# Half of the retention output product by seven products in place of eight, in a two-layer trunk on one core

## The chip, the cores and the metric

The kernel runs on one core of a Trainium2 chip. The metric is the device time of one execution in microseconds. Before the change it is 2571.68 us, the median of three runs (2571.43 to 2574.8). One further execution was profiled; it took 2570.78 us, and its trace spans 2569.0 us from the first to the last instruction.

## The reference

The program is a trunk of two layers over a sequence of 1024 positions with 1024 features. Layer 0 mixes by forgetting attention, layer 1 by retention; each mixer and each feed-forward block (SwiGLU) adds to the residual. The part in question is the end of retention:

```python
    _, y = lax.scan(step, state0, (qc, kc, vc))            # per head: inner + cross
    y = y.transpose(1, 0, 3, 2, 4).reshape(B, S, H, dv)    # H = 4 heads, dv = 512
    mu = jnp.mean(y, axis=-1, keepdims=True)
    var = jnp.mean(jnp.square(y - mu), axis=-1, keepdims=True)
    y = ((y - mu) * lax.rsqrt(var + EPS)).reshape(B, S, H * dv).astype(h.dtype)
    return (jax.nn.silu(g) * y) @ w_out                    # (1024 x 2048) @ (2048 x 1024)
```

So each head gives 512 features per position, normalised over these 512, gated by silu(g), and multiplied by its rows of `w_out`. Four heads make 2048 features, which are 16 feature tiles of 128; heads 0 and 1 are the first eight of them.

## The kernel before

Activations are held transposed: a tile has 128 features in its partitions and 512 positions (one half of the sequence, `H = 512`, called h or ib = 0, 1) along the free axis. Every float32 operand is split into a rounded part and a rest (`hi`, `lo`; ScalarE casts, VectorE subtracts: lines 105 and 106), and a product is three matmuls: hi·hi, hi·lo, lo·hi. A line number is that of the kernel before unless said otherwise.

Retention runs over eight stages (head h, half ib). A stage works in this order: `scores` of the next stage (k times q, L1177 to L1179, then mask and decay on VectorE, L1188 and L1193), `weighted` (v times scores, L1203 to L1205), in the second half `crossed` (state times q, L1214 to L1216), and `finish`. `finish` copies four result banks out (`yt`), squares and adds them (`yacc`, L1233), splits the sum (`ah`, `al`), and adds over the partitions by three matmuls into `sm` (L1238 to L1240); from these come q and fb, and four multiplications `yt * fb` (L1248). For head 0 the gate g is loaded and multiplied there (L1252); for heads 1 to 3 it is multiplied later, in `load_units` (L831), with 1024 columns at once. The result is stored to DRAM as `zd`. `prepare` fetches the next head: kf (k for the transposes L1129), the parts of k and q (L1106, by POOL's queue) and eight v tiles (L1092, by SP's queue, then L1095 and L1096).

The output product then has two halves. The first (heads 0 and 1) takes for each of eight row tiles n a weight of 128x1024, split once, and two halves of eight feature tiles: 8 x 3 matmuls each (`mm_u`, L113 to L115), to which the residual `xo` is added (L1287). The second half (heads 2 and 3) is done by `out_proj` in the same manner, added to the first.

Other products of the kernel already go by seven products of 2x2 blocks (`Products`: matmuls at L675 to L677; `Blocks` forms the sums of the weight's blocks; `Stored` holds the sums of the other operand, B11, B21, B22 as they are and T1 to T4 as sums, in DRAM). For a pair of row tiles and a pair of feature tiles they need 7 products of 128x128x512 where the plain way needs 8.

Tiles come from rings: `units` of the pools bpa (32) and bpb (24) hold the split operands, `yu` 16 tiles of 128x512, `qu` four (`q`; kf lies there too), `st` five of 128x1024, `sc` and `xo` a few. A load waits until the ring's tile has been read for the last time. The order of each engine's instructions is set by the framework's planner, which simulates times while it places them; each engine, and each engine's DMA queue, then works strictly in that order.

Of the kernel before, what the change touches and what calls it, by code (L numbers as in the profile page):

```python
# [17 lines left out]
P = 128  # L18
# [19 lines left out]
def trunk(ctx, tc, nc, d, out):  # L38
# [38 lines left out]
    def yu(s):  # L77
        return yp.tile([P, H], F32, tag="y", name=nm(s))
# [453 lines left out]

    class Combos:
# [74 lines left out]
    class Blocks:  # L608


        def __init__(self, src):
            self.s1, self.ready = None, {}
            sts = []
            for i in range(2):
                st = sp.tile([P, 1024], F32, tag="st", name=nm("st"), bufs=5)
                nc.sync.dma_start(st, src[:, i * 1024:(i + 1) * 1024])
                sts.append(st)
            self.a11, self.a12 = sts[0][:, 0:512], sts[0][:, 512:1024]
            self.a21, self.a22 = sts[1][:, 0:512], sts[1][:, 512:1024]
# [598 lines left out]
    def finish(h, ib, yps):  # L1218
        nc.gpsimd.dma_start(ez.bitcast(F32)[:2, :], ed[:, h * S + ib * H:h * S + (ib + 1) * H])
# [27 lines left out]
        for vt in range(4):  # L1247
            nc.vector.tensor_tensor(ys[vt], ys[vt], fb, op=ALU.mult)  # L1248
            if h < 1:
                g = yu("g")  # L1250
                nc.sync.dma_start(g, gd[4 * h + vt][:, HALF[ib]])
                nc.vector.tensor_tensor(ys[vt], ys[vt], g, op=ALU.mult)  # L1252
            nc.sync.dma_start(zd[4 * h + vt][:, HALF[ib]], ys[vt])

    prepare(0)
# [3 lines left out]
    for i, (h, ib) in enumerate(stages):  # L1259
# [4 lines left out]
        if ib == 1:  # L1264
            crossed(h, yps)
        an = []
# [6 lines left out]
        if ib == 1 and nxt:  # L1273
            heads[h + 1][4] = state(h + 1, heads[h + 1][1], heads[h + 1][3])

    zg = list(zip(zd, [None] * (4 * 1) + gd[4 * 1:]))
    y = [[None, None] for _ in range(KT)]
    acts = [load_units(bpa, *t) for t in zg[:8]]
    for n in range(KT):
        w = wtile2(d["ret_o"][n], 8)  # L1280
        for h in range(2):
            ps = mm_ps()
            mm_u(ps, w, acts, h)
            y[n][h] = yu("y")
            xo = sp.tile([P, H], F32, tag="sc", name=nm("xo"), bufs=4)
            nc.sync.dma_start(xo, xd2[n][:, HALF[h]])
            nc.vector.tensor_tensor(y[n][h], ps, xo, op=ALU.add)  # L1287
    X, nrm, nw = out_proj(d["ret_o"], y, [load_units(bpb if i < 6 else bpa, *t) for i, t in enumerate(zg[8:])], xd, 3, d["ffn_in"][1, 0], MAP3)
# [95 lines left out]
```

## Time and profile before

| What | Number |
|---|---|
| Median of the runs | 2571.68 us |
| The profiled execution | 2570.78 us, span 2569.0 us |
| Granted TensorE clock | 0.999 |
| PE busy | 2546.0 us, 99% |
| DVE busy | 1846.9 us, 72% |
| ACT busy | 1249.9 us, 49% |
| Bytes moved by DMA | 327.92 MB, 128 GB/s on average |
| Retention (1580 to 1775 us) | PE 194.48, DVE 152.23, ACT 120.16 of 195 us |
| First output half (most of it in 1775 to 1880 us) | DVE 33.10 of 55 and 26.72 of 50 us |

PE is the matmul part of TensorE, DVE is VectorE, ACT ScalarE, POOL GpSimd, and SP the engine that issues most DMAs. A row of a timeline has the start, the duration, the engine, the line, the operation, and what it writes and reads; a bracket behind it has the idle time before it and what ended it. Matmuls overlap, so the distance of two starts, not the duration, is what one costs. The times of the profile are those of one execution.

### The profile page before, as it was taken

How to read it: one execution, taken by the hardware profiler on the slowest of the kernel's cores; microseconds unless marked ns; L12 is line 12 of the kernel's file. 1: busy time of each engine (PE TensorE's matmuls, PEld its weight loads, DVE VectorE, ACT ScalarE, POOL GpSimd, SP SyncE). 2: the span in 40 equal slices, each digit the busy share in tenths (PEclk: the TensorE clock that was granted, in tenths of full speed). 3: DMA queues.
4: the chain of work that ended last, by engine and by line, in shares of the span. 5: the costliest groups of instructions: out<-in, count | busy, mean ns of one | idle time of the engine just before them, and what ended most of it. 6: DMA issues, size and time to landing. Idle time of an engine off the chain costs nothing.

```text
span 2569.0 us, 35132 instructions
## 1 busy us (share of the span) xinstructions
PE 2546.0 (99%) x12653; PEld 2165.4 (84%) x12653; DVE 1846.9 (72%) x3093; ACT 1249.9 (49%) x2345; POOL 240.2 (9%) x263
## 2 busy tenths in 40 slices
PE   9999999999999999999999999999999999999998
PEld 8889887888888887889898989888888888888888
DVE  6798888976666768886666566786667666668694
ACT  6566656643333455464444445673354333335543
POOL 0143323000000001001111111210000000000200
PEclk9999999999999999999999999999999999999999
DMA  3111142432332344533343335866522223225541
GB/s 133 44 58 58 58 147 87 156 111 95 114 106 95 122 160 158 175 113 118 109 156 123 128 127 175 277 229 218 193 95 88 106 98 111 105 81 192 169 151 66
DMA packets 145903, 327.92 MB, mean 128 GB/s; under 512 B 17552, under 2 KB 30896, under 8 KB 145728
## 3 DMA queue, kind: packets, MB, share of 16 engines
q1 hardware_dynamic: 136368, 297.79, 33.7%
q0 software_dynamic: 8640, 27.34, 3.1%
q8 instruction: 99, 1.62, 0.3%
q14 instruction: 76, 0.62, 0.1%
q10 hardware_dynamic: 720, 0.55, 0.1%
HBM read 225.44 MB, written 100.17 MB: 127 GB/s over the span
## 4 chain that ended last, share of the span: by engine, by line
PE 94%; DVE 2%; issue 1%; DMA 1%; ACT 1%; POOL 0%; SPq 0%; DVEq 0%; POOLq 0%; ACTq 0%
PE mm L675 19%; PE mm L676 19%; PE mm L677 19%; PE mm L113 7%; PE mm L114 7%; PE mm L115 7%; PE mm L795 2%; PE mm L793 2%; PE mm L794 2%; PE mm L282 1%; PE mm L281 1%; PE mm L280 1%; PE mm L1204 1%; PE mm L1205 1%; PE mm L1203 1%
## 5 line engine op out<-in xcount | busy, mean ns | idle before, releaser
L676 PE MATMUL mm<-b,wh 128*128 128x512 f32 x2128 | 828.0, 389 | 1.2 <-DVE b L106 1.2
L675 PE MATMUL mm<-b,wh 128*128 128x512 f32 x2128 | 825.7, 390 | 1.9 <-DVE 22_1856_9302 L735 1.0
L677 PE MATMUL mm<-b,wl 128*128 128x512 f32 x2128 | 824.3, 389 | 0.0
L105 ACT CAST wh<-st 128x512 fp32r<-128x512 f32 (+4 forms) x450 | 276.1, 615 | 492.6 <-PE mm L676 319.7
L675 PEld LDWEIGHTS mm<-b,wh 128*128 128x128 f32 x2128 | 399.5, 188 | 85.8 <-DVE 22_1856_9302 L735 1.4
L676 PEld LDWEIGHTS mm<-b,wh 128*128 128x128 f32 x2128 | 399.5, 188 | 83.9 <-DVE b L106 1.6
L677 PEld LDWEIGHTS mm<-b,wl 128*128 128x128 f32 x2128 | 399.4, 188 | 83.3 <-DVE wl L106 0.3
L106 DVE TENSOR_TENSOR wl<-st,wh 128x512 fp32r<-128x512 f32 (+4 forms) x450 | 310.8, 695 | 180.2 <-ACT wh L105 171.9
L105 ACT CAST wh<-s 128x512 fp32r<-128x512 f32 x252 | 156.5, 622 | 296.3 <-PE mm L676 261.2
L113 PE MATMUL mm<-b,wh 128*128 128x512 f32 x736 | 285.6, 392 | 7.4 <-ACT b L133 5.1
L114 PE MATMUL mm<-b,wh 128*128 128x512 f32 x736 | 287.0, 390 | 1.7 <-DVE b L106 1.7
L115 PE MATMUL mm<-b,wl 128*128 128x512 f32 x736 | 286.5, 390 | 0.0
L106 DVE TENSOR_TENSOR wl<-s,wh 128x512 fp32r<-128x512 f32 x252 | 180.3, 717 | 103.9 <-ACT wh L105 99.8
L113 PEld LDWEIGHTS mm<-b,wh 128*128 128x128 f32 x736 | 138.4, 188 | 37.3 <-ACT b L133 5.6
L114 PEld LDWEIGHTS mm<-b,wh 128*128 128x128 f32 x736 | 138.5, 188 | 29.5 <-DVE b L106 2.2
L115 PEld LDWEIGHTS mm<-b,wl 128*128 128x128 f32 x736 | 138.5, 188 | 28.3
L794 PE MATMUL mm<-wl,b 128*128 128x256 f32 x448 | 126.4, 283 | 0.0
L793 PE MATMUL mm<-wh,b 128*128 128x256 f32 x448 | 126.2, 283 | 0.0
L795 PE MATMUL mm<-wh,b 128*128 128x256 f32 x448 | 125.9, 283 | 0.0
L523 POOL DMA_DIRECT2D b<-ac_B x24 | 13.3, 553 | 1197.2 <-PE mm L676 1194.6
L627 DVE TENSOR_TENSOR s<-st 128x512 f32<-128x512 f32 x84 | 58.4, 695 | 76.2 <-DMA st<-ffn_in 37.6
L105 ACT CAST b<-st 128x512 fp32r<-128x512 f32 (+1 forms) x136 | 77.8, 606 | 56.0 <-DVE st L831 16.7
(564 smaller groups left out, 4145.5 us busy)
## 6 DMA issues: line engine op xcount, KB each, us to landing
st<-ffn_in SPq DMA_DIRECT2D x88, 512.0 KB, 3.6
st<-ffn_out_pairs SPq DMA_DIRECT2D x32, 512.0 KB, 4.2
ac_T<-t SPq DMA_DIRECT2D x48, 256.0 KB, 2.3
xo<-xd SPq DMA_DIRECT2D x32, 256.0 KB, 2.9
ac_B<-t SPq DMA_DIRECT2D x32, 256.0 KB, 2.5
st<-ac_T SPq DMA_DIRECT2D x16, 512.0 KB, 4.3
b<-ac_T POOLq DMA_DIRECT2D x32, 256.0 KB, 5.7
st<-ret_qk SPq DMA_DIRECT2D x16, 512.0 KB, 4.2
```

Source lines behind the costliest of these rows:

```text
L105: nc.scalar.copy(hi, src)
L106: return nc.vector.tensor_tensor(lo, src, hi.bitcast(F32), op=ALU.subtract)
L113: nc.tensor.matmul(ps, wh, xh, start=(first and k == 0), stop=False, skip_group_check=free)
L114: nc.tensor.matmul(ps, wh, xl, start=False, stop=False, skip_group_check=free)
L115: nc.tensor.matmul(ps, wl, xh, start=False, stop=(last and k == n - 1), skip_group_check=free)
L627: nc.vector.tensor_tensor(self.s1, self.a21, self.a22, op=ALU.add)
L675: nc.tensor.matmul(ps, hi[:, js], th, start=first and j == 0, stop=False, skip_group_check=True)
L676: nc.tensor.matmul(ps, hi[:, js], tl, start=False, stop=False, skip_group_check=True)
L677: nc.tensor.matmul(ps, lo[:, js], th, start=False, stop=(j == 3), skip_group_check=True)
L793: nc.tensor.matmul(o, th[:, tk], hi[:, js], start=f, stop=False, skip_group_check=True)
L794: nc.tensor.matmul(o, th[:, tk], lo[:, js], start=False, stop=False, skip_group_check=True)
L795: nc.tensor.matmul(o, tl[:, tk], hi[:, js], start=False, stop=(j == 3), skip_group_check=True)
```

## The change

The first half of the output product (heads 0 and 1) goes by the seven products, with pairs of row tiles n and pairs of feature tiles j: 4 pairs of rows, each 7 products of 4 x 3 matmuls. For this `finish` forms what `Stored` holds for its four j: in the first half of the sequence it stores the gated tiles as B11 and B21; in the second half it loads these back (into an `st` tile), makes t1, t2 (in `q` tiles), T3 and T4 by four subtractions per j, and stores T1, B22, T2, T3, T4. The gate of head 1 is now multiplied in `finish` too. The weights are read by two DMAs per row tile in pieces of 128 columns (`rows=True`), so that the feature tiles 2j and 2j+1 come apart. The operands of the second half (`Acts`) are loaded one by one during the last pair, as slots come free. The row of constants `ez` is loaded by SP's queue in place of POOL's, and the residual `xo` has two tiles that it shares with `ez` and `mask`.

```diff
+    MAP4 = dict(zip(NAMES, (bpa, bpa, bpb, bpb, bpb, bpa, bpa)))
+    ACTS = {"A11": (6, 7), "S1": (0, 1), "A12": (2, 3), "S3": (4, 5)}
+
+    class Acts:
+        def __init__(self, srcs):
+            self.srcs, self.t = srcs, {}
+
+        def get(self, i):
+            if i not in self.t:
+                self.t[i] = load_units(bpb if i < 6 else bpa, *self.srcs[i])
+            return self.t[i]
...
-        def __init__(self, src):
+        def __init__(self, src, rows=False):
...
-                nc.sync.dma_start(st, src[:, i * 1024:(i + 1) * 1024])
+                if rows:
+                    for t in range(2):
+                        nc.sync.dma_start(st[:, HALF[t]].rearrange("p (j c) -> p j c", j=4), src[i][:, t])
+                else:
+                    nc.sync.dma_start(st, src[:, i * 1024:(i + 1) * 1024])
...
     def finish(h, ib, yps):
-        nc.gpsimd.dma_start(ez.bitcast(F32)[:2, :], ed[:, h * S + ib * H:h * S + (ib + 1) * H])
+        nc.sync.dma_start(ez.bitcast(F32)[:2, :], ed[:, h * S + ib * H:h * S + (ib + 1) * H])
...
-            if h < 1:
-                g = yu("g")
-                nc.sync.dma_start(g, gd[4 * h + vt][:, HALF[ib]])
-                nc.vector.tensor_tensor(ys[vt], ys[vt], g, op=ALU.mult)
-            nc.sync.dma_start(zd[4 * h + vt][:, HALF[ib]], ys[vt])
-
+            if h > 1:
+                nc.sync.dma_start(zd[4 * h + vt][:, HALF[ib]], ys[vt])
+                continue
+            g = yu("g")
+            nc.sync.dma_start(g, gd[4 * h + vt][:, HALF[ib]])
+            nc.vector.tensor_tensor(ys[vt], ys[vt], g, op=ALU.mult)
+            if ib == 0:
+                j = 2 * h + vt // 2
+                nc.sync.dma_start(zc.d[("B11", "B21")[vt % 2]][:, j * H:(j + 1) * H], ys[vt])
+        if h < 2 and ib == 1:
+            for j in (2 * h, 2 * h + 1):
+                js = slice(j * H, (j + 1) * H)
+                e1, o1 = ys[j % 2 * 2:j % 2 * 2 + 2]
+                st = sp.tile([P, 1024], F32, tag="st", name=nm("st"), bufs=5)
+                e0, o0, t1, t2 = st[:, HALF[0]], st[:, HALF[1]], qu("t1"), qu("t2")
+                for t, n in ((e0, "B11"), (o0, "B21")):
+                    nc.sync.dma_start(t, zc.d[n][:, js])
+                nc.vector.tensor_tensor(t1, e1, e0, op=ALU.subtract)
+                nc.vector.tensor_tensor(t2, o1, t1, op=ALU.subtract)
+                nc.vector.tensor_tensor(e1, o1, e1, op=ALU.subtract)
+                nc.vector.tensor_tensor(o0, o0, t2, op=ALU.subtract)
+                for n, t in (("T1", t1), ("B22", o1), ("T2", t2), ("T3", e1), ("T4", o0)):
+                    nc.sync.dma_start(zc.d[n][:, js], t)
+
+    zc = Stored("zc", MAP4, False)
...
+        if i == 7:
+            zc.get("T4")
+            zc.get("B22")
...
-
-    zg = list(zip(zd, [None] * (4 * 1) + gd[4 * 1:]))
+        for n in {5: ("B11", "T1"), 6: ("T2", "B21"), 7: ("T3",)}.get(i, ()):
+            zc.get(n)
...
-    acts = [load_units(bpa, *t) for t in zg[:8]]
-    for n in range(KT):
-        w = wtile2(d["ret_o"][n], 8)
-        for h in range(2):
-            ps = mm_ps()
-            mm_u(ps, w, acts, h)
-            y[n][h] = yu("y")
-            xo = sp.tile([P, H], F32, tag="sc", name=nm("xo"), bufs=4)
-            nc.sync.dma_start(xo, xd2[n][:, HALF[h]])
-            nc.vector.tensor_tensor(y[n][h], ps, xo, op=ALU.add)
-    X, nrm, nw = out_proj(d["ret_o"], y, [load_units(bpb if i < 6 else bpa, *t) for i, t in enumerate(zg[8:])], xd, 3, d["ffn_in"][1, 0], MAP3)
+    acts = Acts(list(zip(zd[8:], gd[8:])))
+    banks[0] += 1
...
+    prod = Products(blocks(0), zc).open()
+    for n in range(KT // 2):
+        u = {q: yu(q) for q in ("11", "12", "21", "22")}
...
+        prod.middle(lambda b: nc.scalar.copy(u["12"], b), closed)
+        nxt = Products(blocks(n + 1), zc, (acts, ACTS) if n == 2 else None).open() if n < 3 else None
+        prod.close()
...
+    X, nrm, nw = out_proj(d["ret_o"], y, [acts.get(i) for i in range(8)], xd, 3, d["ffn_in"][1, 0], MAP3)
```

In the changed program PE has 12522 rows where it had 12570. The change moves instructions in three places that the prediction speaks of.

On DVE, around `al` of finish(1, 0), which the `sm` matmul waits for. In the names, `yt_16012` to `yt_16025` are the results of finish(0, 1), `yacc_16236` and `al_16256` belong to finish(1, 0), `st_16061` and `st_16075` are the tiles loaded back, and L1114 is the v form (L1096 before). Before, the same stretch:

```order
L1248 TENSOR_TENSOR yt_16018<-yt_16018,fb_16032 128x512
L1233 TENSOR_TENSOR yacc_16205<-yacc_16205,sq_16211 128x512
L1252 TENSOR_TENSOR yt_16005<-yt_16005,g_16039 128x512
L1135 SCALAR_TENSOR_TENSOR b_16284<-mm_16278,kap_15354,b_16283 128x256
L1252 TENSOR_TENSOR yt_16008<-yt_16008,g_16044 128x512
L1252 TENSOR_TENSOR yt_16013<-yt_16013,g_16049 128x512
L1252 TENSOR_TENSOR yt_16018<-yt_16018,g_16054 128x512
L1233 TENSOR_TENSOR yacc_16205<-yacc_16205,sq_16216 128x512
L1233 TENSOR_TENSOR yacc_16205<-yacc_16205,sq_16221 128x512
L106 TENSOR_TENSOR al_16225<-yacc_16205,ah_16224 128x512
```

With the change:

```order
L1284 TENSOR_TENSOR t_3089_16062<-yt_16012,st_16061 128x512
L1272 TENSOR_TENSOR yt_16025<-yt_16025,g_16058 128x512
L1114 SCALAR_TENSOR_TENSOR b_16381<-st_16378,vmean_2698_14101,b_16380 128x512
L1114 SCALAR_TENSOR_TENSOR b_16387<-st_16384,vmean_2698_14101,b_16386 128x512
L1251 TENSOR_TENSOR yacc_16236<-yacc_16236,sq_16252 128x512
L1285 TENSOR_TENSOR t_3090_16063<-yt_16015,t_3089_16062 128x512
L1286 TENSOR_TENSOR yt_16012<-yt_16015,yt_16012 128x512
L1284 TENSOR_TENSOR t_3092_16076<-yt_16020,st_16075 128x512
L1114 SCALAR_TENSOR_TENSOR b_16393<-st_16390,vmean_2698_14101,b_16392 128x512
L1287 TENSOR_TENSOR st_16061<-st_16061,t_3090_16063 128x512
L106 TENSOR_TENSOR al_16256<-yacc_16236,ah_16255 128x512
```

Six sums (L1284 to L1287) and the last v loads' operations now stand ahead of `al`; before, they were gates, adds and one transposed k.

In POOL's queue, around the q loads of head 3 (`qd30h` and so on). Before:

```order
L1106 DMA b_16734<-kd31l 128x512
L1219 DMA ez<-ed 2x512
L1106 DMA b_16763<-qd30h 128x512
L1106 DMA b_16764<-qd30l 128x512
L1106 DMA b_16767<-qd31h 128x512
```

With the change (L1124 is L1106 before; L523 loads an operand of the products):

```order
L1124 DMA b_16813<-kd31l 128x512
L523 DMA b_17140<-zcT_15391 128x512
L523 DMA b_17145<-zcT_15391 128x512
L1124 DMA b_16842<-qd30h 128x512
L1124 DMA b_16843<-qd30l 128x512
L1124 DMA b_16846<-qd31h 128x512
```

`ez` has left the queue, and two loads of T1 have come ahead of the q loads.

In SP's queue, around the kf loads for head 2 (kf_10891, kf_10892). Before, they stood among the last stores of the projections:

```order
L1006 DMA qd31l<-m_2805_14700 128x512
L1116 DMA kf_16263<-kf_10891 128x512
L616 DMA st_15208<-ret_g 128x1024
L1120 DMA st_15389<-kd_10875 128x1024
L1006 DMA qd30h<-m_2810_14719 128x512
L1116 DMA kf_16265<-kf_10892 128x512
```

With the change they stand among the stores of the sums (L1289) of finish(0, 1):

```order
L1289 DMA zcT_15391<-t_3089_16062 128x512
L1289 DMA zcB_15394<-yt_16025 128x512
L1289 DMA zcT_15390<-t_3090_16063 128x512
L1289 DMA zcT_15392<-yt_16012 128x512
L1289 DMA zcT_15391<-t_3092_16076 128x512
L1134 DMA kf_16306<-kf_10891 128x512
L1237 DMA ez<-ed 2x512
L1289 DMA zcT_15395<-st_16061 128x512
L1134 DMA kf_16308<-kf_10892 128x512
```

The kf loads have moved back by some eighty rows, behind stores that wait for the sums.

More of the change, by code (lines that the diff above doesn't have):

```diff
@@ L1274, in trunk, with blocks, closed @@
             heads[h + 1][4] = state(h + 1, heads[h + 1][1], heads[h + 1][3])
-    zg = list(zip(zd, [None] * (4 * 1) + gd[4 * 1:]))
+        for n in {5: ("B11", "T1"), 6: ("T2", "B21"), 7: ("T3",)}.get(i, ()):
+            zc.get(n)
     y = [[None, None] for _ in range(KT)]
-    acts = [load_units(bpa, *t) for t in zg[:8]]
-    for n in range(KT):
-        w = wtile2(d["ret_o"][n], 8)
-        for h in range(2):
-            ps = mm_ps()
-            mm_u(ps, w, acts, h)
-            y[n][h] = yu("y")
-            xo = sp.tile([P, H], F32, tag="sc", name=nm("xo"), bufs=4)
-            nc.sync.dma_start(xo, xd2[n][:, HALF[h]])
-            nc.vector.tensor_tensor(y[n][h], ps, xo, op=ALU.add)
-    X, nrm, nw = out_proj(d["ret_o"], y, [load_units(bpb if i < 6 else bpa, *t) for i, t in enumerate(zg[8:])], xd, 3, d["ffn_in"][1, 0], MAP3)
+    acts = Acts(list(zip(zd[8:], gd[8:])))
+    banks[0] += 1
+    def blocks(n):
+        w = [d["ret_o"][2 * n + i][:, :D].rearrange("p (j t c) -> p t j c", t=2, c=P) for i in range(2)]
+        return Blocks(w, True)
+    prod = Products(blocks(0), zc).open()
+    for n in range(KT // 2):
+        u = {q: yu(q) for q in ("11", "12", "21", "22")}
+        def closed(b, c):
+            nc.scalar.copy(u["22"], b)
+            nc.vector.tensor_tensor(u["22"], c, u["22"], op=ALU.add)
+        prod.middle(lambda b: nc.scalar.copy(u["12"], b), closed)
+        nxt = Products(blocks(n + 1), zc, (acts, ACTS) if n == 2 else None).open() if n < 3 else None
+        prod.close()
+        nc.vector.tensor_tensor(u["12"], prod.c, u["12"], op=ALU.add)
+        for i in range(2):
+            for h in range(2):
+                t = u[f"{i + 1}{h + 1}"]
+                xo = sp.tile([P, H], F32, tag="xo", name=nm("xo"), bufs=2)
+                nc.sync.dma_start(xo, xd2[2 * n + i][:, HALF[h]])
+                nc.vector.tensor_tensor(t, ((prod.a, t), (prod.b, t))[i][h], xo, op=ALU.add)
+                y[2 * n + i][h] = t
+        prod = nxt
+    X, nrm, nw = out_proj(d["ret_o"], y, [acts.get(i) for i in range(8)], xd, 3, d["ffn_in"][1, 0], MAP3)
     ffn(1, X, nrm, xd, None, True, nw, MAP3)
```

## The prediction

> **What bounds the kernel now.** I read the page first: the share of each engine, then the chain that ended last.
>
> ```profile
> PE 2546.0 (99%) x12653; PEld 2165.4 (84%) x12653; DVE 1846.9 (72%) x3093; ACT 1249.9 (49%) x2345; POOL 240.2 (9%) x263
> PE 94%; DVE 2%; issue 1%; DMA 1%; ACT 1%; POOL 0%; SPq 0%; DVEq 0%; POOLq 0%; ACTq 0%
> ```
>
> TensorE is busy nearly throughout and carries 94% of the chain. A matmul that goes away is therefore worth its whole pitch, provided that nothing else becomes late. DVE's 72% is an average, so I read it by stage, with busy time per window:
>
> ```profile
> core 0: us, PE busy (x) PEld busy (x) DVE busy (x) ACT busy (x) POOL busy (x), PEclk, DMA share, GB/s
> 1600.00:1610.00 10.00, 9.54 (x46) 7.34 (x45) 10.00 (x24) 7.16 (x17) 4.72 (x9) 1.00 0.90 272
> 1580.00:1775.00 195.00, 194.48 (x1036) 169.90 (x1035) 152.23 (x297) 120.16 (x250) 31.44 (x58) 1.00 0.68 234
> 1775.00:1830.00 55.00, 55.00 (x245) 45.54 (x244) 33.10 (x45) 15.56 (x27) 0.00 (x0) 1.00 0.71 245
> 1830.00:1880.00 50.00, 50.00 (x222) 41.44 (x221) 26.72 (x43) 18.47 (x31) 0.00 (x0) 1.00 0.29 100
> ```
>
> The first row is the one to remember: where DVE is busy for all of 10 us, PE falls to 9.54, the only such place in the stage. The second is retention from the end of the projections to the first output matmuls: DVE works 152 of 195 us there, 78%, and the DMA engines 68%. The last two are the output product; DVE has room there, 33 of 55 and 27 of 50 us. The change puts its sums into the crowded stage.
>
> **Prices.** Starts in PE's timeline give the pitch of a matmul, since the ends overlap:
>
> ```profile
> 1584.75 0.39 PE L677 MATMUL mm<-b,wl 128*128 128x512 f32 x1
> 1584.98 0.39 PE L675 MATMUL mm<-b,wh 128*128 128x512 f32 x1
> 1585.20 0.39 PE L676 MATMUL mm<-b,wh 128*128 128x512 f32 x1
> ...
> 1604.81 0.28 PE L1177 MATMUL mm<-b,b 128*128 128x256 f32 x1
> 1604.93 0.28 PE L1178 MATMUL mm<-b,b 128*128 128x256 f32 x1
> ```
>
> A 128x512 costs 0.227 us and a 128x256 costs 0.12; a 128x384 I put between them at 0.17. DVE's steps come the same way from its timeline in the stage:
>
> ```profile
> 1652.36 0.48 DVE L1193 SCALAR_TENSOR_TENSOR wl<-mm,kap,wh 128x256 fp32r<-128x256 f32 x1
> 1652.75 0.75 DVE L1096 SCALAR_TENSOR_TENSOR b<-st,vmean,b 128x512 fp32r<-128x512 f32 x1
> 1653.41 0.29 DVE L106 TENSOR_TENSOR wl<-atd,wh 128x128 fp32r<-128x128 f32 x1
> 1653.61 0.23 DVE L1185 CAST wl<-zero 128x128 fp32r<-128x128 f32 x1
> 1653.75 0.35 DVE L1193 SCALAR_TENSOR_TENSOR wl<-mm,kap,wh 128x128 fp32r<-128x128 f32 x1
> 1654.01 0.35 DVE L1188 SCALAR_TENSOR_TENSOR atd<-mm,kap,mask 128x128 f32<-128x128 f32 x1
> ...
> 1659.24 2.49 DVE L1248 TENSOR_TENSOR yt<-yt,fb 128x512 f32<-128x512 f32 x4
> 1661.65 0.69 DVE L1233 TENSOR_TENSOR yacc<-yacc,sq 128x512 f32<-128x512 f32 x1
> ```
>
> A 128x512 tensor_tensor costs 0.60 us (four between 1659.24 and 1661.65), the v form 0.66, a 128x256 0.39, a 128x128 0.14 to 0.26.
>
> **Part 1, fewer matmuls.** The first half of the output product had 8 row tiles x 2 halves x 8 feature tiles x 3 = 384 matmuls of 128x512. It now has 4 pairs x 7 products x 12 = 336. 48 x 0.227 = **10.9 us saved**; this is also the most that the change can bring.
>
> **Part 2, the sums of head 0.** They are eight 128x512 operations in finish(0, 1). Their place in DVE's order decides. The matmul of `sm` in finish(1, 0) (now L1258) waits for `al`, and in the new order six of the eight sums, the four gate multiplies, all fb and yt multiplies of finish(0, 1) and seven v loads' operations stand ahead of that `al`. From the first DVE instruction that can only start when the third scores tile of stage (1, 1) is done (an atd) to `al` there are 34 DVE instructions: twenty at 0.60, seven of the v form at 0.66, one 128x256 at 0.39, six small ones for 1.3; together 18.3 us. PE has 50 matmuls between the same two points: fourteen 128x512, three 128x384, thirty-three 128x256; 3.18 + 0.51 + 3.96 = 7.7 us. PE must therefore stand for 18.3 - 7.7 = **10.6 us**, however early anything else is. That this arithmetic can be trusted shows at the one stall before. There the same count over 17 DVE instructions (8.4 us) and 39 matmuls (7.5 us) forces 0.9 us, and PE's rows lose about 1.2: 2.08 us from 1606.33 to 1608.41 for four matmuls that need 0.91.
>
> ```profile
> 1606.33 0.39 PE L1179 MATMUL mm<-b,b 128*128 128x512 f32 x1
> 1607.01 1.37 PE L1203 MATMUL mm<-wh,b 128*128 128x512 f32 x3 [0.30 <-ACT wh L1192]
> 1608.41 0.50 PE L1204 MATMUL mm<-wl,b 128*128 128x512 f32 x1
> ```
>
> Everywhere else in that stage the count came out negative before. The wait is one piece, so three things can lengthen it. Restart of PE: the start of the execution shows it.
>
> ```profile
> 5.11 1.56 PE L113 MATMUL mm<-b,wh 128*128 128x512 f32 x2 [5.11 <-ACT b L133]
> 6.47 0.63 PE L114 MATMUL mm<-b,wh 128*128 128x512 f32 x1
> 6.90 0.63 PE L115 MATMUL mm<-b,wl 128*128 128x512 f32 x1
> 7.32 0.63 PE L114 MATMUL mm<-b,wh 128*128 128x512 f32 x1
> ...
> 8.95 0.39 PE L113 MATMUL mm<-b,wh 128*128 128x512 f32 x1
> ```
>
> After 5.11 us of idle the pitch is 0.43 us until about 8.7; in those 3.6 us about 1.7 are lost. A pause of 10 us is longer than that one: **+1.7** (0 if it takes more than a pause). [...] Next, the kf load for the transposes right behind `sm`. kf and the sums share the four `q` tiles, so kf can no longer be fetched early; its DMA now stands in SP's queue behind the store of a sum (T1 of the second pair), three DVE steps (1.9 us) before `al`. And the g loads:
>
> ```profile
> DMA to landing us min/median/max: 2.5/3.3/4.5
> ...
> 1634.08 10.14 DMA g<-gd
> 1644.31 0.69 DVE yt L1252
> ```
>
> The first is kf's landing: 3.3 - 1.9 = **+1.4** (0.6 to 2.6). The second pair stands in the chain: g took up to 10 us. In the new order the g loads follow a v load that is released 5.9 us of DVE work ahead of the first gate multiply, plus 0.6 of issue: anything from 0 to 4.8; nearer to the low end, since DVE is late here anyway: **+1.5**.
>
> **Part 3, the sums of head 1 and the loads beside them.** The same count from scores of stage (2, 1) to the last `wl` gives 13.2 us of DVE against 13.2 of PE: 0, so this one costs nothing by itself. But the queues lose their lead. kf for head 3 now stands in SP's queue behind a T1 store that waits for a sum, 0.7 us of work before its transposes: 3.3 + 0.3 of issue - 0.7 = **+2.9** (2 to 4). And in POOL's queue the first two T1 operand loads stand ahead of the q loads of head 3; they wait for slots that head 2's last matmuls free, the second of them only 13 matmuls (1.6 us) before the first scores matmul that needs q. Before, q went out with a wide lead:
>
> ```profile
> DMA to landing us min/median/max: 3.5/8.0/11.7
> ...
> 1689.39 0.56 POOL L1106 DMA_DIRECT2D b<-qd30h  x1
> 1689.98 0.55 POOL L1106 DMA_DIRECT2D b<-qd30l  x1
> ...
> 1701.52 0.40 PE L1177 MATMUL mm<-b,b 128*128 128x512 f32 x1
> ```
>
> It was issued at 1689.39 and used at 1701.52: 12 us. That cover is gone. Two issues of 0.55, then a landing of 3.5 to 11.7 us, less 1.6: 3 to 11. Two loads stand ahead of q, not a full queue, so I take 5 for the landing, between the minimum and the median: **+4.5**.
>
> **Part 4, the products.** 28 weight splits in place of 16, 16 operations for block sums, 28 operand splits in place of 16, 24 adds in place of 16: 48 more DVE operations, 29 us, in a phase of 336 x 0.227 = 76 us that kept DVE about 60% busy. The closest count (11 DVE against 28 matmuls) forces 0.2 to 0.8 us, others have 1 to 2 us to spare, and their loads come through the five st tiles: **+2** (0 to 5).
>
> **Part 5, into the second half.** Its eight operand tiles can only be loaded as the last pair frees their slots, and the first plain weight load stands in SP's queue behind a split that a matmul releases 36 matmuls (8.2 us) ahead of its use. Split 0.6, issue 0.3, landing like that of a v tile, cast 0.6:
>
> ```profile
> DMA to landing us min/median/max: 2.9/4.2/11.1
> ```
>
> 4.4 to 12.6 against 8.2 us, with the median below: 0 to 4.4, up to 6 with the act loads; **+2**. The rest of the edit costs nothing: ez on SP has its constant addresses early, zd loses stores that zc replaces, and the gate of head 1 moves from four 1024-wide multiplies to eight half ones, counted above.
>
> **The sum.** -10.9 + (10.6 + 1.7 + 1.4 + 1.5) + (2.9 + 4.5) + 2 + 2 = +15.7 on the profiled execution's 2570.78: 2586.5. The median of the runs, 2571.68, is 0.9 above that execution. I say **2586**. With all unknowns low: 10.6 + 0.6 + 2 + 3 - 10.9 = +5.3, 2576; with all high: 10.6 + 1.7 + 2.6 + 4.8 + 4 + 11 + 5 + 6 - 10.9 = +34.8, 2606.
>
> **Rivals.** (a) *All of DVE's new work stays hidden*: only the saving remains, 2570.8 - 10.9 = 2560. For it speaks that DVE idles 22% of the retention stage; against it the forced 10.6 us, which an average can't undo. (b) *Only the sums of head 0 cost something*, and the loads come in time: -10.9 + 10.6 + 1.7 = +1.4, 2572. For it: a PE that stands 10 us lets every queue catch up, so later waits find DVE and the loads ahead. Against: the two waits of part 3 come a whole stage later and are set by queue order, not by lag. (c) *The loads decide*: the change stores and reloads some 8 MB more through DMA engines that already work 68% of the stage, and reads ret_o in 512-byte pieces; if each landing there rises towards its maximum (4.5, 11.7, 11.1), it is the high sum and more, 2606 or over. This decides once landings exceed about 8 us in the products.
>
> **Chances.** Forecast (2576 to 2602) 0.67, (a) 0.07, (b) 0.14, (c) 0.12. About 0.2%, 5 us, is what a measurement of this kernel can tell from no change. (a) is faster; (b) and a small part of the forecast's low end lie within; so faster 0.08, same 0.14, slower 0.78. The range that leaves out 2 in 10, (a), most of (c) and a little of (b), is 2571 to 2603.
>
> **What would show it.** PE's first row of `sm` in finish(1, 0) should begin with about 10 us or more of idle ended by ACT `ah` or DVE `al`, DVE being busy all that time, with 0.43 pitches behind it; L1195 of stage (3, 0) should wait for DMA b<-qd30h; the transposes L1147 for kf. PE should have 48 rows fewer and the products some 76 us. Wrong would be a forecast in which DVE's steps are shorter than 0.60 beside these loads, or in which the wait at `sm` is under 5 us.

## The result and the profile after

The changed kernel takes 2613.57 us (median of four runs, 2611.16 to 2617.71) against 2572.57 for the kernel before (2571.43 to 2574.8): a ratio of 1.016, interval 1.0148 to 1.0172. It is slower by 41 us, where 14 were forecast: the direction is right, the size is not, and the time lies outside the range. The profiled execution's span grew from 2569.0 to 2609.7 us, by 40.7.

The page of the changed kernel, with the busy time of each engine and the share of the chain that ended last:

```profile
PE 2550.0 (98%) x12605; PEld 2162.6 (83%) x12605; DVE 1883.8 (72%) x3161; ACT 1268.5 (49%) x2381; POOL 252.2 (10%) x283
PE 88%; DVE 5%; DMA 3%; issue 2%; ACT 1%; POOL 0%; SPq 0%; DVEq 0%; POOLq 0%; ACTq 0%
```

The 48 matmuls are gone (12653 to 12605 rows on the page; the program's counts given ahead, 12570 and 12522, differ by the same 48), yet PE's busy time did not fall. DVE has 68 more instructions and the same 72%. PE's share of the chain fell from 94% to 88%, and DVE and DMA took it. The windows say where. First those of the changed kernel (window, its length, then busy time and instructions per engine, granted clock, DMA share, GB/s):

```profile
1648.00:1690.00 42.00, 26.32 (x120) 21.78 (x119) 31.76 (x57) 15.78 (x32) 3.76 (x7) 0.80 0.75 239
1690.00:1750.00 60.00, 48.07 (x254) 41.45 (x253) 38.68 (x78) 29.65 (x63) 8.04 (x15) 0.91 0.76 247
1750.00:1880.00 130.00, 121.02 (x561) 99.30 (x560) 108.29 (x182) 68.84 (x133) 11.86 (x23) 1.00 0.65 218
```

Then the same windows of the kernel before:

```profile
1648.00:1690.00 42.00, 42.00 (x245) 37.94 (x245) 36.46 (x79) 29.31 (x65) 10.73 (x21) 1.00 0.72 246
1690.00:1750.00 60.00, 60.00 (x331) 53.18 (x330) 49.60 (x94) 39.06 (x82) 5.30 (x10) 1.00 0.69 242
1750.00:1880.00 130.00, 130.00 (x575) 107.69 (x574) 77.54 (x115) 42.42 (x73) 0.00 (x0) 1.00 0.51 174
```

PE was busy for the whole of all three. Now it is busy for 26 of 42 us where head 0's sums lie, 48 of 60 at head 1's, and 121 of 130 in the third window, called the products below (it also holds the tail of retention and the start of the second half), where DVE's work has risen from 78 to 108 us. The granted clock is below 1 in the first two.

For a ledger I take the distance between each two starts of PE and subtract the pitch of that shape (0.227, 0.175 and 0.12 us, the medians). What is left over is time lost. In the three windows it was 0.7, 0.7 and 0.4 us before; it is 22.2, 16.5 and 12.5 now. That makes +21.5, +15.8 and +12.1, together +49.4. Less the 48 x 0.227 = 10.9 us saved, +38.5 of the span's +40.7; the other 2 us lie spread over the execution.

The rows behind the ledger, from PE's timeline of the changed kernel (the last bracket is the idle time before the row and what ended it):

```profile
1661.13 0.80 PE L1232 MATMUL mm<-b,b 128*128 128x512 f32 x1 [5.17 <-DVE atd L1206]
...
1674.02 0.79 PE L1256 MATMUL sm<-ah,ones 128*128 128x512 f32 x1 [7.82 <-ACT ah L105]
...
1677.04 0.80 PE L1258 MATMUL sm<-al,ones 128*128 128x512 f32 x1 [1.80 <-DVE al L106]
1678.73 0.69 PE L1147 MATMUL mm<-ident,kf 128*128 128x128 f32 x2 [0.90 <-DMA kf<-kf]
...
1680.07 0.63 PE L1234 MATMUL mm<-b,b 128*128 128x512 f32 x1
1680.50 0.63 PE L1232 MATMUL mm<-b,b 128*128 128x512 f32 x1
...
1730.93 0.69 PE L1147 MATMUL mm<-ident,kf 128*128 128x128 f32 x2 [5.99 <-DMA kf<-kf]
...
1744.65 0.76 PE L1195 MATMUL mm<-b,b 128*128 128x512 f32 x3 [2.95 <-issue]
...
1798.97 0.49 PE L695 MATMUL mm<-b,wl 128*128 128x512 f32 x1 [2.31 <-DVE wl L106]
...
1812.08 0.51 PE L693 MATMUL mm<-b,wh 128*128 128x512 f32 x1 [1.88 <-ACT 12_3468_17560 L1336]
```

The wait at `sm` is there as forecast, 7.82 and 1.80 us. A wait of 5.17 us ahead of it was not forecast. Behind the long waits the starts are 0.43 us apart (1680.07 to 1680.50) in place of 0.227. The profile names no releaser for the row 1744.65; the q load that it reads (qd30h) was issued on POOL's queue at 1741.14, behind the second T1 load of 1740.52, and landed at 1744.56.

Where the 5.17 comes from stands in DVE's timeline:

```profile
1657.30 0.75 DVE L1114 SCALAR_TENSOR_TENSOR b<-st,vmean,b 128x512 fp32r<-128x512 f32 x1 [6.09 <-ACT b L1113]
...
1658.17 0.34 DVE L1206 SCALAR_TENSOR_TENSOR atd<-mm,kap,mask 128x128 f32<-128x128 f32 x1
...
1676.30 0.68 DVE L106 TENSOR_TENSOR al<-yacc,ah 128x512 fp32r<-128x512 f32 x1
...
1792.81 0.69 DVE L645 TENSOR_TENSOR s<-st 128x512 f32<-128x512 f32 x1 [3.30 <-DMA st<-ret_o]
```

DVE itself stood for 6.09 us, until a v tile came. From its `atd` at 1658.17 it then worked without a gap until `al` ended at 1676.98: 18.8 us, where 18.3 had been counted. (Five of the eight sums stand ahead of that `al`, not six as said ahead; the count of twenty operations at 0.60 us is right with five.) The last row belongs to the products: there DVE stood 3.30 us for a weight. The v tile was late because of SP's queue, whose DMA issues follow:

```profile
1646.31 0.32 SPq L1283 DMA_DIRECT2D st<-zcB  x1
1646.72 0.38 SPq L1275 DMA_DIRECT2D zcB<-yt  x1
...
1651.31 0.32 SPq L1283 DMA_DIRECT2D st<-zcB  x1
1651.72 1.33 SPq L1110 DMA_DIRECT2D st<-vd  x3
```

L1283 is the reload of B11 and B21. A reload goes out only when its store (L1275) has landed, and the v loads of the next head (L1110) stand behind it. The reload went out at 1651.31 and the v loads at 1651.72. The chain of waits shows the landing that this waited for (4.51 us from 1646.72), and the same again a stage later:

```profile
1646.72 4.51 DMA zcB<-yt
...
1687.35 6.50 DMA zcB<-yt
1693.86 0.32 SPq L1283
1694.23 7.65 DMA st<-vd
1701.90 0.73 ACT b L1113
...
1724.78 6.11 DMA kf<-kf
```

From the store of 1687.35 to the v tile it takes 14.5 us.

### The profile page after: what moved, and what is told of

It is laid out like the page before. It is cut to its first block, busy times and chain, and to the rows that moved or that the text cites. A ratio compares the mean times of both kernels' runs of the same rounds, so it can differ in the third digit from the quotient of the medians.

```text
span 2609.7 us, 35230 instructions
## 1 busy us (share of the span) xinstructions
PE 2550.0 (98%) x12605; PEld 2162.6 (83%) x12605; DVE 1883.8 (72%) x3161; ACT 1268.5 (49%) x2381; POOL 252.2 (10%) x283
## 4 chain that ended last, share of the span: by engine, by line
PE 88%; DVE 5%; DMA 3%; issue 2%; ACT 1%; POOL 0%; SPq 0%; DVEq 0%; POOLq 0%; ACTq 0%
PE mm L693 19%; PE mm L694 19%; PE mm L695 19%; PE mm L113 6%; PE mm L114 6%; PE mm L115 6%; PE mm L813 2%; PE mm L811 2%; PE mm L812 2%; PE mm L282 1%; PE mm L281 1%; PE mm L280 1%; DVE b L106 1%; PE pv L387 0%; PE pv L388 0%
## 5 line engine op out<-in xcount | busy, mean ns | idle before, releaser
L105 ACT CAST wh<-s 128x512 fp32r<-128x512 f32 x264 | 163.9, 622 | 312.0 <-PE mm L694 273.3
L106 DVE TENSOR_TENSOR wl<-s,wh 128x512 fp32r<-128x512 f32 x264 | 188.0, 714 | 106.6 <-ACT wh L105 102.3
L523 POOL DMA_DIRECT2D b<-ac_B x24 | 13.2, 551 | 1191.6 <-PE mm L694 1189.5
L105 ACT CAST b<-st 128x512 fp32r<-128x512 f32 (+1 forms) x120 | 69.1, 605 | 47.7 <-DMA st<-ac_T 12.7
```

Of the source, the lines that this page charges most:

```text
L105: nc.scalar.copy(hi, src)
L106: return nc.vector.tensor_tensor(lo, src, hi.bitcast(F32), op=ALU.subtract)
```

## The experiments

Four causes could make up the 41 us: the *amount* of DVE's new work, the *place* of the sums ahead of `al`, the *queue* (store, reload and v loads in one order), and the *loads* themselves (bytes, 512-byte pieces). All times below are medians beside the kernel before on the same chip, which lay between 2572.7 and 2573.1 us each time; the edits are made to the changed kernel unless said otherwise. The planner orders every edited kernel anew, so other instructions move too: a share that is read from the difference of two runs holds the change of order with it.

**e1: the sums without the reload.**

```diff
-                for t, n in ((e0, "B11"), (o0, "B21")):
-                    nc.sync.dma_start(t, zc.d[n][:, js])
-                nc.vector.tensor_tensor(t1, e1, e0, op=ALU.subtract)
+                nc.vector.tensor_tensor(t1, e1, o1, op=ALU.subtract)
...
-                nc.vector.tensor_tensor(o0, o0, t2, op=ALU.subtract)
+                nc.vector.tensor_tensor(o0, o1, t2, op=ALU.subtract)
```

> The two loads that bring a head's first-half tiles back (L1283, eight DMAs) are left out; the sums are made from the second half's tiles, so the number of VectorE operations and of stores is that of the change, but the sums' values are not. Queue theory (each reload waits in SP's queue for its store to land, and the v and g loads behind it wait too: 6 us of VectorE's wait in stage (0, 1), as much again a stage later): 15 to 18 us less than the change's 2613.6, so 2596 to 2599, and no wait of 6 us for a v tile ahead of the sums. VectorE theory (the sums' 0.60 us each decide and the reload lies beside them): less than 5 us gained, 2609 or more.

Measured: 2602.22 us (2601.13 to 2604.29), ratio 1.0112 (1.0096 to 1.0127). PE's timeline of e1:

```profile
1666.20 0.79 PE L1256 MATMUL sm<-ah,ones 128*128 128x512 f32 x1 [5.82 <-ACT ah L105]
1668.57 0.79 PE L1258 MATMUL sm<-al,ones 128*128 128x512 f32 x1 [1.14 <-DVE al L106]
1671.27 0.69 PE L1147 MATMUL mm<-ident,kf 128*128 128x128 f32 x2 [1.91 <-DMA kf<-kf]
```

11.4 us less than the change, between what the two theories gave. The first wait of 5.17 is gone; head 0's window loses 14.1 us in place of 22.2. Part 2 had priced 13.7 without the g loads (10.6 + 1.7 + 1.4); that the two agree is partly chance, since the waits at `sm` are 7.0 us here in place of 10.6 and the one for kf is longer. So the reload explains some 11 of the 41 us, and 29 remain without it.

**e2: neither reload nor sums in retention.**

```diff
-                st = sp.tile([P, 1024], F32, tag="st", name=nm("st"), bufs=5)
...
-                nc.vector.tensor_tensor(o0, o0, t2, op=ALU.subtract)
-                for n, t in (("T1", t1), ("B22", o1), ("T2", t2), ("T3", e1), ("T4", o0)):
+                for n, t in (("T1", e1), ("B22", o1), ("T2", e1), ("T3", o1), ("T4", e1)):
```

> Reloads and the sixteen sums are both left out; the same tiles are stored unsummed in their place, and the products run as in the change (the values are not the reference's). What remains is the price of the product phase, of T1 ahead of q, and of the stores. Queue theory and VectorE theory together: the stalls at sm and kf vanish, 2613.6 - 22 - 3 - 10 = about 2578, of which 11 us are the product phase and the way into the second half. If the stores or the pieces of 512 bytes are what slows the stage, it stays above 2595.

Measured: 2580.5 us (2576.55 to 2586.77), 1.0028 (1.0019 to 1.0037). Its windows of head 0 and of the products:

```profile
1648.00:1690.00 42.00, 41.52 (x235) 37.43 (x236) 38.62 (x83) 26.00 (x58) 8.60 (x16) 1.00 0.85 299
...
1750.00:1880.00 130.00, 119.77 (x505) 96.86 (x504) 95.94 (x149) 57.93 (x102) 1.64 (x4) 0.96 0.58 196
```

Retention is whole again: 0.8, 1.3 and 0.3 us are lost in its stretches (1648 to 1690, to 1720 and to 1750 us), at a DMA share of 0.85, higher than before and after the change. The products are not: 16.4 us are lost there, at waits such as the following in e2's PE timeline:

```profile
1830.18 0.80 PE L693 MATMUL mm<-b,wh 128*128 128x512 f32 x1 [4.53 <-ACT 22_3557_17996 L1325]
```

L1325 copies a result bank out. On ScalarE it stands behind casts for the operands of the second half, which wait for their gate loads (the chain ahead of the row has such a load of 6.37 us). So the 16 sums and the reload carry 33 us, and the products lose more than the whole saving by themselves; 16.4 us, where 11 were expected for them and the way into the second half.

**e3: the sums only after the next `al`.**

```diff
+                with tc.issue_after(als[h + 1, 0]):
+                    nc.vector.tensor_tensor(t1, e1, e0, op=ALU.subtract)
...
-        finish(h, ib, yps)
+        after = finish(h, ib, yps)
+        if pend:
+            pend()
+        pend = after
```

> The sums of a head may only be issued on VectorE behind al of the next stage; nothing else is changed and the output is the reference's. Place theory (the sums cost because they stand ahead of al, as the prediction put it): the 10.6 us of stage (0, 1) go, 2600 to 2604. Amount theory (VectorE has no room in this stretch, wherever the sums stand): the wait moves to the transposed k tiles behind it, where the order forces 9.3 us, and the time stays within 5 us of 2613.6.

Measured: 2619.64 us (2615.57 to 2622.31), 1.0173 (1.0156 to 1.019). The wait moved. PE's timeline of e3:

```profile
1676.27 0.80 PE L1258 MATMUL sm<-ah,ones 128*128 128x512 f32 x1 [6.37 <-ACT ah L105]
...
1690.12 0.69 PE L1147 MATMUL mm<-ident,kf 128*128 128x128 f32 x2 [12.20 <-DMA kf<-kf]
```

The wait at `sm` only falls from 7.82 to 6.37, the one ahead of it stays (5.15 us), and kf, which shares the `q` tiles with the sums, is now 12.20 us late, where the order forced 9.3. So the place ahead of `al` alone is not the cause: what stands behind the sums pays. The time is 6 us above the change, a little outside what the amount theory gave.

**e4: e3, and the reloads issued behind the last v load of the head after next** (`vlast[h + 2]`; the sums are called behind that head's `prepare`).

```diff
+                with tc.issue_after(vlast[h + 2]):
+                    for t, n in ((e0, "B11"), (o0, "B21")):
+                        nc.sync.dma_start(t, zc.d[n][:, js])
```

> The reloads are issued on SP only behind the last v load of the head after next, and the sums behind al of the next head's first half; all is computed. Queue theory: with the v and g loads no longer behind the reloads the stalls of stages (0, 1) and (1, 1) shrink to what VectorE's total forces (4.6 us in 104) plus kf and q, so 2585 to 2592. VectorE theory: 2605 or more.

Measured: 2587.96 us (2587.78 to 2590.97), 1.0058 (1.0043 to 1.0073), 25.6 less than the change. This is the best that the change came to with all its work in it, and still 15 us slower than before. PE's timeline of e4 has one long wait left in retention, which its chain leads back to a v load of 9.15 us:

```profile
1685.61 0.58 PE L1197 MATMUL mm<-b,b 128*128 128x256 f32 x1 [6.30 <-ACT yt L1246]
```

Retention loses 11.5 us (8.9 + 2.0 + 0.6), the products 14.6. Together with e1 and e3 this points to the order in SP's queue for the first share of retention's loss. Moving the reload behind the v loads, with the sums behind the next `al`, gains 14 us more than leaving it out with the sums where they were; so place does count once the queue is free. How the 14 us divide between the two was not taken apart.

**e9: the reloads by POOL's queue**, `nc.sync` to `nc.gpsimd` in the reload alone.

> The change with one word altered: the reloads are issued by POOL's queue in place of SP's. All traffic and all VectorE work stay, and the output is the reference's; the forced wait at sm is 10.0 us. Queue theory (the reloads cost because the v and g loads stand behind them on SP): as much is won as by leaving them out, 2600 to 2606. Traffic theory (their bytes cost): within 4 us of the change's 2613.6. On POOL's queue one reload of head 1 now stands ahead of the q loads of head 2, so a new wait there is possible, up to 5 us.

Measured: 2616.1 us (2615.22 to 2617.32), 1.0168 (1.0152 to 1.0185). The gain that the queue theory gave did not come; the time is where the traffic theory put it. PE's timeline of e9:

```profile
1673.53 0.79 PE L1256 MATMUL sm<-ah,ones 128*128 128x512 f32 x1 [10.28 <-ACT ah L105]
...
1695.14 0.89 PE L1195 MATMUL mm<-b,b 128*128 128x512 f32 x4 [3.32 <-DMA b<-qd20h]
```

The v loads go out earlier, by 1646.48, and the first wait falls from 5.17 to 2.21 us. But in the chain of waits they land after 7.7 and 6.4 us, where the change's landed after 4.8 us from 1651.72, and the wait at `sm` grows. POOL's q loads now stand behind a reload that goes out only at 1687.68, and are late. So e9 does not separate the queue from the traffic.

**e11: a reload of data that had long been stored** (gate tiles), so that only its dependency on the store goes.

```diff
-                for t, n in ((e0, "B11"), (o0, "B21")):
-                    nc.sync.dma_start(t, zc.d[n][:, js])
+                for k, t in enumerate((e0, o0)):
+                    nc.sync.dma_start(t, gd[2 * j + k][:, HALF[0]])
```

> The change, but the eight reloads read gate tiles that have long lain in DRAM in place of the tiles just stored (the sums' values are not the reference's). Bytes, st tiles, SP's queue and VectorE's work are those of the change; only the wait of a load for its own store is gone. Queue theory (that wait, with the v and g loads behind it, is what the reload costs): as much is won as by leaving the reloads out, 2600 to 2605. Traffic theory (bytes and st tiles cost): within 4 us of 2613.6.

Measured: 2607.68 us (2603.95 to 2610.59), 1.0136 (1.012 to 1.0151): 6 us less than the change. This lies between what the two theories gave. In head 0's window the wait of 5.17 is gone and 13.9 us are lost, as in e1, so there the dependency on the store accounts for all that e1 won. But 17.5 us are lost at head 1, where e1 loses 13.0: the waits for kf (5.52 us) and q (3.22) are those of the change, and so not due to the dependency, while e1's order issues kf at 1714.16 (1724.78 in the change) and waits at other places. So the dependency is about half of the reload's 11.4 us. Whether the other half is its bytes, the `st` tile that it holds or the changed order was not taken apart.

**e5: ret_o read by whole rows**, one DMA in place of two in 512-byte pieces.

```diff
-                    for t in range(2):
-                        nc.sync.dma_start(st[:, HALF[t]].rearrange("p (j c) -> p j c", j=4), src[i][:, t])
+                    nc.sync.dma_start(st, src[i])
```

> The change, with the weight of each row tile read by one DMA of whole rows in place of two in pieces of 512 bytes (eight DMAs fewer; the feature tiles of a pair then do not belong together, so the output is not the reference's). Nothing else is changed and the forced stall at sm is the same 10.7 us. Load theory (rival c: the small pieces and the DMA engines' load decide): at least 8 us less than 2613.6. Queue and VectorE theories: within 4 us of it, since the wait for these weights in the change's profile is one of 3.3 us.

Measured: 2610.45 us (2607.5 to 2612.63), 1.0149 (1.0132 to 1.0166), 3.1 less than the change. DVE's wait for a weight falls from 3.30 to 0.72 us, and the products' wait of 2.31 at 1798.97 goes with it; the waits at the bank copies stay. So the pieces cost about 2 of the 12 us that the products lose, and are not what the rest waits for.

**e6: e4 with the 16 sums on GpSimd**, and **e7: also the sums of the weight's blocks there** (`nc.vector` to `nc.gpsimd` in these lines).

> As with the v loads first (reloads behind the v loads), and the sixteen sums are made by GpSimd in place of VectorE; all is computed. VectorE theory: the retention stage loses what is left of its stalls but for v loads that wait for st tiles, about 5 of its 10 us; the product phase keeps its own (the order forces 8.2 us between the last stage and the third product), so 2580 to 2586. If GpSimd takes over 1.5 us a sum, or slows VectorE beside it, kf and T1 come later and it is not under 2588.

> As the one before, and the sixteen sums of the weight's blocks in this product are made by GpSimd too; the order then forces no more than 0.9 us anywhere on VectorE. If VectorE's amount is what the product phase waits for, the 14 us of it fall to 5 and the time to 2570 to 2576, the first that is not slower than before; if the products wait for copies and banks (ACT) or for loads instead, it stays at that of the run before, within 3 us.

Measured: e6 2593.4 us (2592.55 to 2597.08), 1.0084 (1.0069 to 1.0099); e7 2602.47 us (2601.76 to 2604.91), 1.0118 (1.0103 to 1.0133). Both are slower than e4. In retention's groups of e6, GpSimd takes 1.5 to 1.6 us for what DVE does in 0.6 (count, then busy time and mean ns):

```profile
L1289 POOL TENSOR_TENSOR t<-yt,st 128x512 f32<-128x512 f32 x4 | 6.5, 1634 | 41.4 <-DMA g<-gd 40.8 <-DVE yt L1276 0.6
L1276 DVE TENSOR_TENSOR yt<-yt,g 128x512 f32<-128x512 f32 x16 | 15.3, 969 | 9.6 <-DMA g<-gd 9.4
```

The second row is DVE's gate multiply, 684 ns on average in the change and 969 here. In e7 one form of block sum took 3.0 us on GpSimd, and the products lost 27.6 us. As a test of the amount this is spoiled, since GpSimd's slower steps became late themselves.

**e10: e4 without the 16 block sums in this product.** This takes 16 operations out of DVE's work, and also out of the way from a weight's load to its cast and split.

```diff
         def sums(self, early=False):
+            if self.rows:
+                self.s1, self.s2 = self.a21, self.a22
+                return
...
-                nc.vector.tensor_tensor(self.s2, self.a12, self.s2, op=ALU.subtract)
+                if not self.rows:
+                    nc.vector.tensor_tensor(self.s2, self.a12, self.s2, op=ALU.subtract)
```

> As with the v loads first (2588.0), but the sums of the weight's blocks in this product are left out (unsummed blocks take their place, so the output is not the reference's): 16 VectorE operations, 9.6 us, fewer in the product phase. VectorE's amount theory: PE's loss in the product phase, 14.5 us with the v loads first, falls to 6 or less, and the time to 2578 to 2581. If the phase waits for copies of banks that stand on ACT behind casts, or for loads: 2584 to 2590.

Measured: 2580.15 us (2577.42 to 2581.96), 1.0027 (1.0016 to 1.0039): 7.8 us less than e4 for 16 operations of 0.6, that is 9.6 us of DVE's work. The window of the products, of e4 and then of e10:

```profile
1750.00:1880.00 130.00, 119.83 (x522) 96.33 (x521) 104.81 (x164) 62.41 (x112) 7.00 (x13) 0.99 0.61 204
```

```profile
1750.00:1880.00 130.00, 125.65 (x558) 102.46 (x557) 98.16 (x152) 65.60 (x117) 7.02 (x13) 1.00 0.64 213
```

The loss in the products falls from 14.6 to 6.7 us. Four fifths of the time taken off DVE come back on PE, in a stretch where DVE is busy for 105 of 130 us. PE's waits for a weight's cast or split (`wh`, `wl`) fall from 6.2 to 0.6 us; those at bank copies hardly change (4.2 and 3.9). Whether the amount of DVE's work or the longer way of the weight counts more, e10 can't tell.

**e12: e2 and e10 together: no sums at all.**

> As without sums and reloads (2580.5), and the sums of the weight's blocks are left out too: 32 VectorE operations, 19.2 us, fewer than the change, all matmuls, stores and operand loads as in it (values not the reference's). Amount theory: another 6 to 9 us less, 2571 to 2575, so that the seven products still gain at most a part of their 10.9 us, since 28 operand splits in place of 16 and 28 weight splits in place of 16 remain. If the product phase waits for banks and loads instead: 2578 or more.

Measured: 2573.8 us (2570.9 to 2578.47), 1.0008 (0.9999 to 1.0017). With 48 matmuls fewer and 32 DVE operations less than the change it only comes level with the kernel before. Its products still lose 11.0 us, the whole saving. What remains there are 24 more splits, 8 more adds on DVE and 12 copies of result banks on ScalarE that the kernel before did not have. The trace shows three long waits of PE, each for a bank to be read out: 1.88 us at 1771.81 for a copy that stands on ScalarE behind two steps of the last `finish` (q), 1.92 at 1776.74 for an add that stands on DVE behind four multiplications of it (yt), and 2.33 at 1824.47 for a copy behind casts that wait for gate loads, as in e2; behind the last the pitch is 0.43 us for a while. DVE was idle for part of the time before two of these waits, so here it is the order in which the banks are read out, more than the amount; no run changed that order alone.

Taken off one after another, the reload (e1) gave 11.4 us, the 16 sums (e1 to e2) 21.7 and the 16 block sums (e2 to e12) 6.7, and 2573.8 is left. The order matters for the shares: with the reload moved instead (e4), the same 16 sums and the reload together cost 7.5 us over e2.

**e8: the kernel before with 24 operations added to DVE in finish(1, 0)**, to measure the count of Part 2 by itself.

```diff
         hi, lo = yr("ah"), yr("al")
+        if (h, ib) == (1, 0):
+            for _ in range(24):
+                nc.vector.tensor_tensor(acc, acc, acc, op=ALU.max)
```

> The kernel before, with 24 more 128x512 VectorE operations in finish(1, 0) that leave the sum of squares as it is (maximum with itself); no DMA is added and nothing else changes. The same count as in the prediction forces 10.0 us: 33 VectorE instructions of 18.2 us against 8.2 us of matmuls. If the count and the restart are right: one wait of about 10 us, behind it matmuls at 0.43 us for 1.7 us more, 2572.7 + 11 to 13 = 2584 to 2586. If PE makes up for such a wait later: under 2580. If a restart costs nothing: 2582 to 2583.

Measured: 2591.08 us (2589.31 to 2591.68), 1.0071 (1.0056 to 1.0086), +18.3 where 11 to 13 were expected. PE's timeline of e8, then DVE's:

```profile
1695.73 0.80 PE L1241 MATMUL sm<-ah,ones 128*128 128x512 f32 x1 [5.53 <-ACT ah L105]
...
1699.20 0.79 PE L1203 MATMUL mm<-wh,b 128*128 128x512 f32 x1 [1.82 <-ACT yt L1224]
```

```profile
1685.61 0.35 DVE L1188 SCALAR_TENSOR_TENSOR atd<-mm,kap,mask 128x128 f32<-128x128 f32 x1
...
1687.80 7.22 DVE L1238 TENSOR_TENSOR yacc<-yacc 128x512 f32<-128x512 f32 x10
1695.71 0.69 DVE L106 TENSOR_TENSOR al<-yacc,ah 128x512 fp32r<-128x512 f32 x1 [0.68 <-ACT ah L105]
```

Each operation reads the result of the one before it, and ten took 7.22 us, 0.72 each and not 0.60. With the other runs of such operations (four in 2.87, two in 1.41) the 24 come to about 16.3 us, 1.9 more than counted. The one wait of about 10 us did not come. By start distances PE waits six times, for 1.1, 1.9, 5.7, 2.2, 1.8 and 1.2 us, together 13.9, and only the first three, 8.7, stand ahead of `al`. So e8 does not confirm the 10.0. A count from another place does fit: the `atd` of 1685.61 reads a scores tile whose last matmul started at 1685.18. From there to the end of `al` at 1696.40 DVE takes 10.8 us (0.68 of it idle), and PE has 3.1 us of matmuls; 7.7 are forced, and the two waits there are 1.9 and 5.7, together 7.6. In this trace the 33 instructions reach back to 1676.74 and 8.2 us of matmuls only to 1680.5, so the two sides of the 10.0 do not start at one point. The rest of the 17.4 us that PE loses, 3.5, is mostly slow pitch behind the waits, not the 1.7 of one restart.

## Why the prediction was wrong in size

With every unknown at its high end the prediction's sum came to 2606, so the 2613.6 needs terms that were not in it. The two largest: at head 0 the late start of DVE's chain had no term, and in the products the waits at copies of result banks had none.

**The saving** is as forecast: 48 rows fewer, 10.9 us.

**Part 2, head 0** (15.2 forecast, 21.5 measured). The count itself held: DVE took 18.8 us for the 34 instructions counted at 18.3, and PE had the 50 matmuls counted at 7.7. The kf term held too (1.5 against 1.4). The 1.5 for the g loads did not appear: DVE had no gap there. Two things failed, both beside the count:
- The count bounds the wait only from the moment DVE begins. DVE stood 6.1 us before its chain, because the reload waits in SP's queue for its store to land and the v loads stand behind it. So PE lost 17.5 us between the first of the 50 matmuls (1651.88) and the last, where 10.6 were forecast. I had counted the stores and reloads only as bytes in rival (c), and this wait was in no term. e11 shows it: without the dependency the wait of 5.17 is gone and head 0 loses 13.9 us in place of 22.2. It is a wait added to SP's queue whose followers I did not list. (The waits at `sm` alone are 8.0 + 2.2 = 10.2 us by start distances. That this is so near to 10.6 is partly chance: some of the counted wait lies in the 5.17 ahead of it.)
- The restart was counted once, with 1.7 us. There were two slow stretches, 1661 to 1664 and 1674 to 1685, and they lost about 5 us. The first, 1.6 us, cost nothing of its own, since PE waited for DVE behind it in any case; behind `al` the second lost 2.9. The granted clock was 0.83 from 1660 to 1670, 0.56 from 1670 to 1680 and 0.76 from 1680 to 1690, and each of the waits of 5.2 and 7.8 us at head 0 and of 6.0 us at head 1 is followed by the 0.43 pitch. Of the shorter waits in the last section one is followed by it and two are not. The loss per slow stretch is 1.6 to 3.3 us here.

**Part 3, head 1** (7.4 forecast, 15.8 measured). Both mechanisms were right: the transposes wait for kf, and q is issued behind the T1 loads and is late at L1195. The kf term was mis-sized: its landing was taken as 3.3 us and took 6.11, the wait 6.15 in place of 2.9. The q wait is 3.1 in place of 4.5, with a landing of 3.4 where 5 was taken. What was missing are the waits for `ah`, `wl` and `wh` (1.35, 1.3 and 0.67 us), which come from v loads held up by the second store and reload, and another restart of 2.5 us.

**Parts 4 and 5, the products and the way into the second half** (4 forecast, 12.1 measured). I costed the products by the closest count over short chains of DVE's steps (0.2 to 0.8 us) and took the rest of DVE's room for granted ("a phase that kept DVE about 60% busy"). That step failed in three ways. First, the 12 bank copies on ScalarE were in no term, and waits for them (L702, L1333, L1336) make up 5.1 of the 12.1 us. Second, DVE stood 3.30 us for a weight (row 1792.81) and then worked without a gap for more than 20 us, and a split (row 1798.97) and a copy on ScalarE (row 1812.08, behind a cast that waits for a block sum) come late in that stretch. With whole rows (e5) the wait at 1798.97 is gone, and without the block sums (e10) 9.6 us less of DVE's work gave 7.8 us back. Third, the last `finish` and the gate loads of the second half stand in the same queues ahead of copies and adds that free the banks, as e2 and e12 show. The waits don't stay with the instructions added. How the 12.1 divide among these was not taken apart.

**The rivals.** (a), all hidden, fell: PE stood. (b), only head 0, fell: the waits at head 1 and in the products came as well. Though PE stood for 17 us at head 0, the queues did not catch up. (c) gave the nearest number, 2606 or over, by a mechanism that is at most a part of it: in e2 the DMA engines were at 85% at head 0 and retention lost 2.4 us in all, and e5 took away the pieces for 3 us. Long landings do appear (kf 6.11, a v tile 7.65 us), and e9 leaves room for traffic beside the queue.

## What to carry to other kernels

A count of one engine's work against another's between two points fitted the waits here, 17.5 us at head 0 (18.8 - 7.7 and 6.1 of late start make 17.2) and 7.6 against 7.7 in e8, but only with the start of the chain known and both sides counted from the same point; what may delay that start has to be looked for in every queue that the change puts a wait into. A load of what has just been stored, put into an in-order queue, holds up everything behind it for the landing of the store (4.5 and 6.5 us here), and moving it behind the urgent loads, together with the sums, won 25.6 us, where moving the sums alone lost 6. And seven products for eight save an eighth of the matmuls, 10.9 us here, for 64 more sums, splits and adds on an engine with little room: even with every sum left out the change only came level.

## What the runs showed of the hardware

The slow pitch after a pause (0.43 us in place of 0.227) did not end after a fixed time. After the waits of 7.8 and 1.8 us it lasted from 1674 to 1684.8, with short waits in between, and after the wait of 6.0 us from 1731.3 to 1735.9, both longer than the 3.6 us seen at the start of the execution.

Nor did it take a long wait. PE's timeline of e12, in the products:

```profile
1824.47 0.50 PE L698 MATMUL mm<-b,wh 128*128 128x512 f32 x1 [2.33 <-ACT 22_3551_17978 L1330]
...
1826.24 0.63 PE L698 MATMUL mm<-b,wh 128*128 128x512 f32 x1
1826.66 0.63 PE L699 MATMUL mm<-b,wh 128*128 128x512 f32 x1
```

After a wait of 2.33 us the first starts are 0.23 to 0.34 us apart, and those from 1825.81 to 1828.80 are 0.43 apart. Yet behind the waits of 2.31 and 2.95 us in the change (rows 1798.97 and 1744.65) the granted clock is 1.00, from 1798 to 1803 and from 1744 to 1748 us. What decides between them the runs do not show.

Beside GpSimd's sums some of DVE's instructions grew long and others did not. DVE's timeline of e6, while GpSimd did sums without a gap:

```profile
1677.24 0.34 DVE L1208 SCALAR_TENSOR_TENSOR atd<-mm,kap,mask 128x128 f32<-128x128 f32 x1
1677.51 1.51 DVE L1116 SCALAR_TENSOR_TENSOR b<-st,vmean,b 128x512 fp32r<-128x512 f32 x1
1678.94 1.34 DVE L106 TENSOR_TENSOR wl<-atd,wh 128x128 fp32r<-128x128 f32 x1
1680.21 0.34 DVE L1208 SCALAR_TENSOR_TENSOR atd<-mm,kap,mask 128x128 f32<-128x128 f32 x1
```

`wl` took 1.34 us in place of 0.28 and the v form 1.51 in place of 0.75, while `atd`, which reads a result bank (`mm`), kept its 0.34. The last of these sums ended at 1681.41; the next `wl`, at 1682.14, took 0.28 again and the next v form, at 1682.74, 0.73. What makes some of the instructions long and leaves others as they are the runs do not show.
